# Bias rows stored three heads at a time, and a last block that loads all low words of its weights

## The chip, the core and the metric

The kernel runs on one core of a Trainium2 chip. The metric is the device time of one execution in microseconds. The median of three timed runs of the kernel before is 3193.27 us (3175.7 to 3194.81).

## What is computed

One streaming step of a one-layer hybrid encoder, for a prompt of 2048 rows and a sample of 8 x 16 rows, width 1024, all in float32. Two head groups share one input projection; the bias of this case belongs to the second.

```python
h = rmsnorm(x, norm1_g) * (1 + sc1) + sh1          # modulated by silu(c) @ w_mod + b_mod
proj = h @ w_in                                    # one projection, columns split between the groups
o_a, conv_state, s = mixer_a(...)                  # gated DeltaNet: 4 heads x 128, conv of 4, chunked delta rule
o_b = band_attention(qb, kb, vb, rel_bias)         # 8 heads x 64; 64-row chunks read 8 chunks back
#   rel_bias (8, 320): d = clip(qpos - kpos, -63, 256) + 63;  scores += rel_bias[:, d]
x = x + g1 * (concat(o_a, o_b) @ w_out)
h = rmsnorm(x, norm2_g) * (1 + sc2) + sh2
x = x + g2 * (square(relu(h @ w_up)) @ w_down)
```

## The kernel before

**Products in three passes.** Every weight is cut into a high word (a cast by ScalarE, L175) and a low word (raw minus high), and each product is made of three matmuls: high by high, high by low, low by high (`mm3`, L161 to L164; L519 to L521). `weights` (L166) loads one raw tile of 512 or 528 KB into one of three buffers of the tag raw, casts it into one of four buffers of the tag w, and then gets the low word in one of two ways. The first time that a tile of w_in is used, in block 0, GpSimd subtracts (L182) and SP stores the low word in the DRAM tensor s_w_in (L184). Later the low word is loaded from there (L179).

**Stage one** works through the 17 row tiles in six blocks (`BLOCKS1`): three tiles each, block 0 with the sample tile, block 5 with two. The text counts blocks from one where it says "block two to four" (numbers 1 to 3 in the code) and "last block" (number 5). Each block runs `proj_a` (gate columns, then queries, keys and values of the four heads of group A) and `proj_b` (the columns of group B); blocks 2 and 4 have their `proj_b` put off to the end, so that the order at the end is proj_a of 4, proj_a of 5, then proj_b of 5, 4 and 2. In the last block the flag `mix` makes every other call of `weights` subtract on GpSimd, though the low word is stored: 14 of its 28 tiles. Beside the projections, steps of the delta rule of the block before are interleaved: A is stored and loaded as 32 x 32 pieces (`s_A`, `Z`, `s_U`, A at L666), and VectorE inverts them (`solve32`). While the last blocks run, the first attention tiles already go (`attention_first`), with `bias` read from s_bias.

**The bias rows.** `rel_bias` (L1092) loads the 8 x 320 table into `ext`, writes on VectorE a reversed and extended row of 768 elements for each head on partitions 32 to 39 (L1098 to L1100), stores it in s_ext (L1101), and then copies from DRAM to DRAM, with a step of -1 from row to row, the bias of a tile of 128 rows by 640 columns for each head into s_bias (L1102, 8 x 128 rows of 2,560 bytes) and the sample's 16 by 528 into s_bs (L1103). The tile comes from the tag big, whose two buffers nothing else uses so early.

**What sets the order.** The code is written once in program order; the tile framework then schedules it by a timeline of its own and by when buffers come free, so instructions can go well ahead of where the code has them. `rel_bias` is called ahead of block 1 in the code; its transfers and copies stand in block 0 in the built program. All transfers but a few are issued by SP, in one queue and in order: an issue that must wait holds all those behind it. The engines, too, each work in order.

## Time and profile before

| | |
|---|---|
| timed runs | 3193.27 us median (3175.7 to 3194.81) |
| profiled execution, device time | 3181.62 us |
| profiled execution, span from first to last instruction | 3179.9 us |
| TensorE matmul rows, busy | 3046.9 us, 96% |
| VectorE / ScalarE / GpSimd, busy | 55% / 46% / 20% |
| mean granted clock of TensorE | 0.985 |
| stage one, up to the first product with w_out | about 1114 us of the span |

Busy time is the union of an engine's instructions. A row of waits gives an engine that stood idle, the instruction that it then ran, and the one whose end let it run. Rows of SPq are issues: how long SP took to get a transfer out, not how long it ran. "DMA share" in a stretch is the mean busy share of the 16 transfer engines.

### The profile page before, as it was taken

The page shows a single profiled execution, that of the slowest core. Times are in us where ns is not written, and L with a number is a line of the kernel's source. Part 1 is how long each engine was busy: PE and PEld are TensorE (multiplying, and loading weights), DVE is VectorE, ACT ScalarE, POOL GpSimd, SP SyncE. Part 2 cuts the span into 40 slices and gives each one's busy share as a digit, 9 for nine tenths or more (in the row PEclk, how much of TensorE's full clock was granted, in tenths as well). Part 3 has the DMA queues.
Part 4 walks back from the last instruction along what each step waited for, and adds up shares of the span by engine and source line. Part 5 has one row for each costly group of instructions (what it writes and reads, how often), then busy time and mean ns, then how long its engine had stood idle before and what let it go on. Part 6 is the DMA issues. An engine that isn't in the chain of part 4 may idle for free.

```text
span 3179.9 us, 52984 instructions
## 1 busy us (share of the span) xinstructions
PE 3046.9 (96%) x19649; PEld 2701.7 (85%) x19649; DVE 1764.0 (55%) x4222; ACT 1472.8 (46%) x2803; POOL 644.5 (20%) x517
## 2 busy tenths in 40 slices
PE   6999999999889989999999999999999999999998
PEld 4998989899889878888999888888988877888887
DVE  4775677667878663674356752454745433442223
ACT  3654545555466555545455353444354333333222
POOL 3631211121342247653222200000000000000000
PEclk9999999999999989999999999999999999999999
DMA  8798897888788778876777765666666676856654
GB/s 289 239 294 268 258 284 228 253 250 248 234 268 264 214 229 277 254 250 231 253 238 244 238 214 181 197 193 204 232 198 200 214 236 219 273 173 194 193 190 139
DMA packets 625947, 735.88 MB, mean 231 GB/s; under 512 B 59328, under 2 KB 483248, under 8 KB 623640
## 3 DMA queue, kind: packets, MB, share of 16 engines
q1 hardware_dynamic: 619928, 701.03, 70.1%
q0 software_dynamic: 5760, 31.46, 3.0%
q8 instruction: 155, 2.54, 0.3%
q14 instruction: 104, 0.85, 0.1%
HBM read 619.74 MB, written 115.52 MB: 231 GB/s over the span
## 4 chain that ended last, share of the span: by engine, by line
PE 70%; DMA 13%; DVE 9%; issue 3%; ACT 3%; POOL 1%; SPq 1%; POOLq 0%; ACTq 0%; DVEq 0%
PE psu L1483 7%; PE psu L1482 7%; PE psu L1484 7%; PE psd L164 7%; PE psd L162 7%; PE psd L163 7%; PE psb L163 2%; DMA raw<-in_w_up_dram 2%; PE psb L162 2%; PE psb L164 2%; PE pv L1286 2%; PE psS L1268 2%; PE psq L519 1%; PE psq L521 1%; PE psq L520 1%
## 5 line engine op out<-in xcount | busy, mean ns | idle before, releaser
L175 ACT CAST w<-raw 128x1024 fp32r<-128x1024 f32 (+1 forms) x528 | 552.1, 1047 | 387.1 <-PE psd L164 214.1
L1482 PE MATMUL psu<-hT,w 128*128 128x512 f32 (+2 forms) x1328 | 470.1, 356 | 1.9 <-ACT hT L104 1.7
L1484 PE MATMUL psu<-hT,w 128*128 128x512 f32 (+2 forms) x1328 | 468.5, 354 | 1.4 <-DMA w<-s_w_up 1.4
L1483 PE MATMUL psu<-hT,w 128*128 128x512 f32 (+2 forms) x1328 | 469.2, 354 | 0.4 <-DVE hT L82 0.3
L82 POOL TENSOR_TENSOR w<-raw,w 128x1024 fp32r<-128x1024 f32 (+1 forms) x162 | 391.6, 2427 | 351.3 <-ACT w L175 285.3
L162 PE MATMUL psd<-w,u 128*128 128x512 f32 x1088 | 430.9, 396 | 0.4 <-DVE y L82 0.3
L164 PE MATMUL psd<-w,u 128*128 128x512 f32 x1088 | 429.8, 396 | 0.0
L163 PE MATMUL psd<-w,u 128*128 128x512 f32 x1088 | 426.8, 392 | 2.1 <-POOL w L82 2.1
L79 DVE SCALAR_TENSOR_TENSOR psu<-psu,r 128x512 f32<-128x512 f32 (+2 forms) x160 | 98.9, 618 | 447.0 <-ACT r L92 446.9
L82 DVE TENSOR_TENSOR y<-y,psd 128x512 f32<-128x512 f32 x238 | 162.4, 685 | 260.3 <-PE psd L164 259.3
L1484 PEld LDWEIGHTS psu<-hT,w 128*128 128x128 f32 x1328 | 250.5, 189 | 33.2 <-DMA w<-s_w_up 1.7
L1482 PEld LDWEIGHTS psu<-hT,w 128*128 128x128 f32 x1328 | 250.1, 189 | 33.0 <-ACT hT L104 2.5
L1483 PEld LDWEIGHTS psu<-hT,w 128*128 128x128 f32 x1328 | 250.7, 189 | 31.9 <-issue 1.3
L92 ACT ACTIVATE r<-psu 128x512 f32<-128x512 f32 (+2 forms) x160 | 85.4, 534 | 375.7 <-issue 214.0
L163 PEld LDWEIGHTS psd<-w,u 128*128 128x128 f32 x1088 | 204.6, 188 | 47.8 <-POOL w L82 2.8
L164 PEld LDWEIGHTS psd<-w,u 128*128 128x128 f32 x1088 | 204.2, 188 | 46.4 <-issue 0.4
L162 PEld LDWEIGHTS psd<-w,u 128*128 128x128 f32 x1088 | 204.4, 188 | 43.8 <-DVE y L82 1.0
L162 PE MATMUL psb<-w,hT 128*128 128x256 f32 x816 | 236.0, 290 | 0.9 <-ACT hT L104 0.8
L163 PE MATMUL psb<-w,hT 128*128 128x256 f32 x816 | 234.7, 288 | 0.9 <-DMA w<-s_w_in 0.9
L164 PE MATMUL psb<-w,hT 128*128 128x256 f32 x816 | 233.4, 286 | 1.9 <-DVE hT L82 1.8
L519 PE MATMUL psq<-hT,w 128*128 128x384 f32 (+1 forms) x576 | 196.9, 342 | 8.1 <-ACT ba L499 8.1
L521 PE MATMUL psq<-hT,w 128*128 128x384 f32 (+1 forms) x576 | 193.6, 336 | 0.2 <-DMA w<-s_w_in 0.2
(315 smaller groups left out, 6459.5 us busy)
## 6 DMA issues: line engine op xcount, KB each, us to landing
raw<-in_w_up_dram SPq DMA_DIRECT2D x160, 512.0 KB
raw<-in_w_down_dram SPq DMA_DIRECT2D x160, 512.0 KB
raw<-in_w_in_dram SPq DMA_DIRECT2D x156, 512.0 KB
w<-s_w_down SPq DMA_DIRECT2D x128, 512.0 KB
w<-s_w_in SPq DMA_DIRECT2D x117, 512.0 KB
w<-s_w_up SPq DMA_DIRECT2D x96, 512.0 KB
raw<-in_w_out_dram SPq DMA_DIRECT2D x40, 512.0 KB
x<-in_x_prompt_dram SPq DMA_DIRECT2D x38, 512.0 KB
```

The costliest lines, as they stand in the source:

```text
L79: (eng or self.nc.vector).scalar_tensor_tensor(out, in0, scalar, in1, op0, op1)
L82: (eng or self.nc.vector).tensor_tensor(out, in0, in1, op)
L92: self.nc.scalar.activation(out, in_, func, **kw)
L162: mm(out, lh, rh, start=first, stop=False)
L163: mm(out, lh, rl, start=False, stop=False)
L164: mm(out, ll, rh, start=False, stop=last)
L175: nc.scalar.copy(w[:, 0, 0:n], r)
L519: mm(pc, wh, hT[:, k, 0, 0:T], start=(k == 0), stop=False)
L521: mm(pc, wl, hT[:, k, 0, 0:T], start=False, stop=(k == KT - 1))
L1482: mm(ps[:, c0:c1], wh, h2[:, k, 0, c0:c1], start=(k == 0), stop=False)
L1483: mm(ps[:, c0:c1], wh, h2[:, k, 1, c0:c1], start=False, stop=False)
L1484: mm(ps[:, c0:c1], wl, h2[:, k, 0, c0:c1], start=False, stop=(k == KT - 1))
```

## The change

`rel_bias` takes a range of heads and is called three times, in blocks 1, 2 and 3 of the code, for three, three and two heads. Its tile now comes from the tag htmp (512 columns a partition), so the extended row lies in two parts on two groups of partitions: three copies and a memset for each call, and two stores to s_ext. The s_bias and s_bs stores cover the heads of the call. In `weights` the flag `mix` and its counter go: a low word that is stored is always loaded, so the 14 subtracts of the last block become 14 loads.

```diff
@@ -174,12 +174,11 @@
         nc.sync.dma_start(r.rearrange("p (a b) -> p a b", a=a), src)
         nc.scalar.copy(w[:, 0, 0:n], r)
         key, kept = (name, k0, c0), self.s_w[name]
-        self.turn += self.mix
-        if key in self.stored and not (self.mix and self.turn % 2):
+        if key in self.stored:
             nc.sync.dma_start(w.bitcast(F32)[:, 1, 0:n], kept[self.stored[key]][:, 0:n])
             return v(0), v(1)
         self.tt(w[:, 1, 0:n], r, w[:, 0, 0:n].bitcast(F32), ALU.subtract, eng=nc.gpsimd)
-        if self.keep[name] and key not in self.stored:
+        if self.keep[name]:
             m = sum(k[0] == name for k in self.stored)
             nc.sync.dma_start(kept[m][:, 0:n], w.bitcast(F32)[:, 1, 0:n])
             self.stored[key] = m
@@ -1058,10 +1057,9 @@
             for bi, tiles in enumerate(B):
                 self.bi = bi
                 self.keep["w_in"] = bi == 0
-                if bi == 1:
-                    self.rel_bias()
+                if 1 <= bi <= 3:
+                    self.rel_bias(3 * bi - 3, min(3 * bi, BH))
                 self.drain_to(bi - 2)
-                self.mix = bi == last
                 blk = self.proj_a(tiles, self.hT, B[bi + 1] if bi in LATE else ())
                 if bi == last:
                     break
@@ -1079,7 +1077,6 @@
             rest = [last] + list(LATE)
             self.pace(0.85 * sum(cb(b) for b in rest))
             for b, nb in zip(rest, rest[1:] + [None]):
-                self.mix = b == last
                 self.proj_b(B[b], self.hT, B[nb] if nb is not None else ())
             self.drain()
             nc.sync.dma_start(self.o["gdn_prompt"][0, 0].rearrange("h k v -> k h v"), self.S)
@@ -1089,18 +1086,23 @@
         self.ap2 = self.ctx.enter_context(tc.tile_pool(name="p2att", bufs=1, space=bass.MemoryType.PSUM, side="right"))
 
 
-    def rel_bias(self):
-
-        nc = self.nc
-        x = self.hp.tile([P, D], F32, tag="big", name="ext", bufs=2)
-        ext, rev = x[0:BH, 0:REL], x[32:32 + BH, 0:EXT]
-        nc.sync.dma_start(ext, self.i["rel_bias"][0])
-        nc.vector.memset(rev[:, EXT - 64:], 0.0)
-        nc.vector.tensor_copy(rev[:, EXT - 64 - REL:EXT - 64], ext[:, ::-1])
-        nc.vector.tensor_copy(rev[:, 0:EXT - 64 - REL], bcast(ext[:, REL - 1], 1, EXT - 64 - REL))
-        nc.sync.dma_start(self.s_ext, rev)
-        nc.sync.dma_start(self.s_bias, dram_ap(self.s_ext, P, [[EXT, BH], [-1, P], [1, 640]]))
-        nc.sync.dma_start(self.s_bs, dram_ap(self.s_ext, P, [[EXT, BH], [-1, SL], [1, 528]]))
+    def rel_bias(self, h0, h1):
+
+        nc = self.nc
+        m, k = h1 - h0, EXT - 64 - REL
+        x = self.hp.tile([P, 4, P], F32, tag="htmp", name="ext", bufs=2).rearrange("p a b -> p (a b)")
+        ext, lo, hi = x[0:m, 0:REL], x[32:32 + m], x[64:64 + m, 0:EXT - 512]
+        rev = ext[:, ::-1]
+        nc.sync.dma_start(ext, self.i["rel_bias"][0][h0:h1])
+        nc.vector.tensor_copy(lo[:, 0:k], bcast(ext[:, REL - 1], 1, k))
+        nc.vector.tensor_copy(lo[:, k:], rev[:, 0:512 - k])
+        nc.vector.tensor_copy(hi[:, 0:EXT - 576], rev[:, 512 - k:])
+        nc.vector.memset(hi[:, EXT - 576:], 0.0)
+        nc.sync.dma_start(self.s_ext[h0:h1, 0:512], lo)
+        nc.sync.dma_start(self.s_ext[h0:h1, 512:], hi)
+        o = h0 * EXT + P
+        nc.sync.dma_start(self.s_bias[h0:h1], dram_ap(self.s_ext, o, [[EXT, m], [-1, P], [1, 640]]))
+        nc.sync.dma_start(self.s_bs[h0:h1], dram_ap(self.s_ext, o, [[EXT, m], [-1, SL], [1, 528]]))
 
     def softmax(self, ap, ps, bias, n):
 
@@ -1558,7 +1560,7 @@
     def run(self):
         self.nraw, self.nw = 3, 4
         self.deferred, self.lanes, self.pending, self.fill_rate, self.fill_acc = [], ([], [], []), [0, 0, 0], 0.0, 0.0
-        self.slot, self.mix, self.turn = 0, False, 0
+        self.slot = 0
         self.front, self.solved, self.spent = 0, 0, 0
         self.constants()
         self.phase1()
```

The instructions' order, as the scheduler has built it, is shown in three places. The first is SP's queue in block 0, around the second to sixth weight tile (`s_w_in<-w` is the store of a low word, `sg` the gate's rows). Before:

```order
45 L373 DMA x<-in_x_prompt_dram 128x1024
46 L184 DMA s_w_in<-w 128x1024
47 L174 DMA raw<-in_w_in_dram 128x8x128
48 L1102 DMA s_bias<-s_ext 1024x1x640
49 L1103 DMA s_bs<-s_ext 128x1x528
50 L297 DMA mrow<-in_b_mod_dram 9x256
51 L184 DMA s_w_in<-w 128x1024
52 L174 DMA raw<-in_w_in_dram 128x8x128
53 L373 DMA x<-in_x_prompt_dram 128x1024
```

Of the changed kernel, the same place in the same queue:

```order
43 L372 DMA x<-in_x_prompt_dram 128x1024
44 L183 DMA s_w_in<-w 128x1024
45 L174 DMA raw<-in_w_in_dram 128x8x128
46 L296 DMA mrow<-in_b_mod_dram 9x256
47 L183 DMA s_w_in<-w 128x1024
48 L174 DMA raw<-in_w_in_dram 128x8x128
49 L372 DMA x<-in_x_prompt_dram 128x1024
```

The two stores of the bias are gone from between the weight tiles (as are the ext load and the s_ext store a few rows earlier). The second place is SP's queue early in block two, where the delta rule of the first block stores `s_U` and loads A back. Before:

```order
160 L771 DMA s_U<-Ds 768x1x32 x2
161 L500 DMA s_sg<-sgw 128x256
162 L174 DMA raw<-in_w_in_dram 128x8x128
163 L179 DMA w<-s_w_in 128x1024
164 L174 DMA raw<-in_w_in_dram 128x8x128
165 L179 DMA w<-s_w_in 128x1024
166 L666 DMA A<-s_U 32x4x32 x12
167 L560 DMA s_kt<-kvw 128x128 x3
168 L179 DMA w<-s_w_in 128x1024
```

Of the changed kernel, from the s_ext stores of the first three heads on:

```order
159 L1101 DMA s_ext<-ext 3x512
160 L1102 DMA s_ext<-ext 3x256
161 L499 DMA s_sg<-sgw 128x256
162 L174 DMA raw<-in_w_in_dram 128x8x128
163 L178 DMA w<-s_w_in 128x1024
164 L174 DMA raw<-in_w_in_dram 128x8x128
165 L178 DMA w<-s_w_in 128x1024
166 L174 DMA raw<-in_w_in_dram 128x8x128
167 L1104 DMA s_bias<-s_ext 384x1x640
168 L1105 DMA s_bs<-s_ext 48x1x528
169 L665 DMA A<-s_U 32x4x32 x12
171 L178 DMA w<-s_w_in 128x1024
```

The stores of three heads now stand between the weight tiles and the twelve loads of A. The third place is GpSimd in the last block (`r`, `nk`, `rq` and `zs` are small powers, `X` and `Ds` products of the delta rule). Before:

```order
157 L82 TENSOR_TENSOR w<-raw,w 128x1056
158 L296 MEMSET mrow 128x256
159 L101 TENSOR_TENSOR r<-r,cpow 128x1 x2
160 L101 TENSOR_TENSOR nk<-ssk,cpow 128x12
161 L101 TENSOR_TENSOR rq<-ssq,cpow 128x12
162 L82 TENSOR_TENSOR w<-raw,w 128x1024 x2
163 L82 TENSOR_TENSOR X<-X,nk 128x512
164 L82 TENSOR_TENSOR ta<-low_342,g 128x512
165 L82 TENSOR_TENSOR Ds<-E,strict_339 128x512
166 L82 TENSOR_TENSOR w<-raw,w 128x1024
```

Of the changed kernel, the same place on GpSimd:

```order
154 L101 TENSOR_TENSOR r<-r,cpow 128x1
155 L295 MEMSET mrow 128x256
156 L101 TENSOR_TENSOR nk<-ssk,cpow 128x12
157 L101 TENSOR_TENSOR rq<-ssq,cpow 128x12
158 L101 TENSOR_TENSOR r<-r,cpow 128x1
159 L82 TENSOR_TENSOR X<-X,nk 128x512
160 L82 TENSOR_TENSOR ta<-low_342,g 128x512
161 L82 TENSOR_TENSOR Ds<-E,strict_339 128x512 x2
```

The subtracts of raw tiles are gone from between the small products; on SP a row `w<-s_w_in` stands for each.

## Rows read from the trace of the kernel before

**Rows 1.** The page, part 1: busy us, share of the span, instructions.
```profile
PE 3046.9 (96%) x19649; PEld 2701.7 (85%) x19649; DVE 1764.0 (55%) x4222; ACT 1472.8 (46%) x2803; POOL 644.5 (20%) x517
```

**Rows 2.** Timeline of SP's queue from 50 us: start, us, the issue.
```profile
50.38 0.84 SPq L1102 DMA_DIRECT2D s_bias<-s_ext  x1
51.28 8.49 SPq L1103 DMA_DIRECT2D s_bs<-s_ext  x1
...
61.88 0.39 SPq L174 DMA_DIRECT2D raw<-in_w_in_dram  x1
62.39 5.70 SPq L373 DMA_DIRECT2D x<-in_x_prompt_dram  x1
```

**Rows 3.** Timeline of ScalarE, 62 to 79 us; idle before and releaser in brackets.
```profile
74.43 1.04 ACT L175 CAST w<-raw 128x1024 fp32r<-128x1024 f32 x1 [6.82 <-DMA raw<-in_w_in_dram]
...
78.46 0.17 ACT L499 COPY ba<-psg 128x8 f32<-128x8 f32 x1 [1.75 <-DVE sgw L79]
```

**Rows 4.** Waits of TensorE, 40 to 80 us: total us, times, longest.
```profile
PE psq L519 <- ACT ba L499: 8.1, 1, 8.1
PE psh L346 <- ACT htmp L92: 3.7, 1, 3.7
```

**Rows 5.** Timeline of VectorE, 40 to 49 us.
```profile
40.76 2.60 DVE L1099 COPY ext<-ext 8x320 f32<-8x320 f32 x1 [2.25 <-DMA ext<-in_rel_bias_dram]
43.28 2.48 DVE L1100 COPY ext<-ext 8x384 f32<-8x384 f32 x1
...
45.90 0.40 DVE L89 TENSOR_SCALAR htmp<-psh,modT 128x128 f32<-128x128 f32 x1
...
48.99 0.48 DVE L1051 MEMSET S<- 128x512 f32 x1 [0.17 <-DVE modT L324]
```

**Rows 6.** Busy time by stretch, with its column line.
```profile
core 0: us, PE busy (x) PEld busy (x) DVE busy (x) ACT busy (x) POOL busy (x), PEclk, DMA share, GB/s
56.00:62.00 6.00, 4.52 (x30) 3.84 (x29) 4.50 (x11) 2.92 (x7) 0.56 (x1) 1.00 0.53 209
250.00:260.00 10.00, 8.10 (x50) 7.07 (x48) 2.92 (x6) 5.16 (x11) 0.00 (x0) 0.66 1.02 278
640.00:757.00 117.00, 116.80 (x870) 112.32 (x869) 87.18 (x260) 60.88 (x139) 16.67 (x17) 1.00 0.88 267
757.00:870.00 113.00, 104.83 (x939) 94.07 (x938) 91.94 (x255) 59.79 (x147) 41.54 (x28) 1.00 0.75 218
870.00:935.00 65.00, 58.22 (x493) 52.50 (x491) 47.82 (x142) 37.51 (x80) 29.18 (x26) 0.92 0.87 262
```

**Rows 7.** Timeline of ScalarE, 250 to 404 us.
```profile
251.18 1.04 ACT L175 CAST w<-raw 128x1024 fp32r<-128x1024 f32 x1 [5.63 <-DMA raw<-in_w_in_dram]
...
402.08 0.16 ACT L526 COPY psq<-hist 128x3 f32<-128x3 f32 x1 [2.20 <-PE psq L521]
402.18 1.05 ACT L175 CAST w<-raw 128x1024 fp32r<-128x1024 f32 x1
```

**Rows 8.** Timeline of SP's queue, 228 to 250 us.
```profile
231.54 8.22 SPq L666 DMA_DIRECT2D A<-s_U  x12
```

**Rows 9.** Waits of ScalarE, 480 to 520 us.
```profile
ACT w L175 <- PE psg L164: 2.8, 2, 2.0
```

**Rows 10.** Groups of GpSimd's instructions, 757 to 906 us: busy us, mean ns.
```profile
L82 POOL TENSOR_TENSOR w<-raw,w 128x1024 fp32r<-128x1024 f32 (+1 forms) x14 | 34.0, 2432 | 37.0 <-ACT w L175 31.9 <-DMA mrow<-in_b_mod_dram 4.2 <-POOL ss L101 0.8
```

**Rows 11.** Timeline of all engines, 885 to 892 us.
```profile
884.91 0.41 DVE L82 TENSOR_TENSOR qraw<-qraw,ss 128x256 f32<-128x256 f32 x1
...
889.78 2.42 POOL L82 TENSOR_TENSOR w<-raw,w 128x1024 fp32r<-128x1024 f32 x1 [0.82 <-POOL ss L101]
889.88 2.61 DVE L82 TENSOR_TENSOR qraw<-qraw,ss 128x256 f32<-128x256 f32 x1
892.41 0.41 DVE L313 COPY mrow<-ptm 9x256 f32<-9x256 f32 x1
```

**Rows 12.** Waits of TensorE, 757 to 935 us.
```profile
PE pS L845 <- DVE w L82: 3.3, 1, 3.3
...
PE ptq L554 <- DVE vT L79: 1.6, 2, 1.1
...
PE ptk L1011 <- DVE mrow L313: 1.3, 1, 1.3
PE psg L162 <- DVE kq L79: 1.1, 1, 1.1
```

## The prediction

> **What bounds the kernel now.** The page's busy line comes first: the TensorE matmul rows cover 96% of the span and no other engine is near that [rows 1]. So a microsecond counts only where TensorE waits, or where work that is taken away had been stopping it. I therefore read the waits of TensorE in the two places that the change touches, then the engines that it waits for there, then SP's queue, which issues nearly all transfers in order and stands still whenever one of its issues cannot go out. The reader is to see three things. At the start of the kernel TensorE waits 8.1 and 3.7 us in two single waits, and both lead back to the bias rows [rows 2 to 5]. Where the change puts the bias rows, TensorE is busy but the transfers are close to full. In the last block VectorE is the engine that TensorE waits for, while GpSimd subtracts beside it; those rows come below with their terms.
>
> **What is taken from the start.** SP issues the store of s_bias at 50.38 us; the s_bs store behind it then holds the queue for 8.49 us, and an x load a little later for 5.70, where an ordinary issue takes 0.39 [rows 2]. That is 13.4 us in which SP was held, and the weight load at 61.88 stands behind the first of the two holds. ScalarE, which casts weights in its program order, waits 6.82 us for a raw tile and only then reaches the small copies that free the sums of the first gate tiles [rows 3]; the matmul behind them waits 8.1 us [rows 4]. The other wait, 3.7 us, is that of the transposes that build hT. VectorE had spent 40.76 to 45.8 us on two copies of ext, and the htmp row that the transposes need comes behind them at 45.90 [rows 5]. With both causes gone I take off both waits, 8.1 + 3.7 = 11.8 us, and call it 12. The next thing to be late is the following raw tile, since the weights are cut in two for the first time here and each also has to be stored; that is why I don't go beyond 12. If the transfers of this stretch were the limit by themselves, only the 3.7 us and part of the 8.1 would go: 6 us is the lower bound, about half.
>
> **What is put into blocks two, three and four.** Per block SP gets five transfers (the ext load, two parts of s_ext, s_bias and s_bs), so 15 in all for the old 4. VectorE gets three copies and a memset on two or three partitions. The two copies of before took 2.60 and 2.48 us while GpSimd was subtracting, and a memset 0.48 [rows 5]; GpSimd is nearly idle in the new places (0.00 us busy in 250 to 260 [rows 6]), so I take the lower value, some 2 us for the four on an engine that has idle time there, and nothing on the path. The stores are the question. In 56 to 62 us, with SP held and little but the s_bias rows under way, the transfer engines are busy at a share of 0.53 and move 209 GB/s [rows 6]. So the old store ran at half of the engines' capacity: 2.62 MB (8 heads of 128 rows of 2,560 bytes) at 209 GB/s is 12.5 us. Two readings fit. If half of the engines is what any such store gets, three heads (0.98 MB) take 4.7 us. If it is one engine for each head (8 of 16), three heads get 3 of 16, and 0.98 MB at 3/8 of 209 GB/s takes 12.5 us again; two heads on 2 engines as well. Then the 13 us are not divided by three but paid three times, each time on few engines, and since every weight load is spread over the engines, each load behind the store waits for the slow ones. The exact half speaks for the second reading, and I use it.
>
> The Trainium skill speaks for it too ("DMA: Bandwidth & Descriptors", section "Why a DMA increments its semaphore by 16 and not by 1"): a transfer uses the largest number of engines up to 16 that divides the slowest dimension of both its patterns. The trace agrees as far as it goes, with 0.53 for a pattern whose slowest dimension is 8. By that rule the new stores run on 3, 3 and 2 engines, and the sum is the one made here; by bytes alone each store would be over in about 3 us and the sum would be the first rival's.
>
> What such an event costs TensorE is bounded below by 0 and above by what the same 13 us cost at the start, 8.1 us [rows 4]; three times that is 24.3. Block two is the nearest to the start: its store stands ahead of twelve A loads and the next weight loads on SP. In the kernel before ScalarE already waits 5.63 us for a raw tile at 251 us [rows 7], and TensorE's granted clock falls to 0.66 in 250 to 260 [rows 6]; the A loads, whose issue takes 8.22 us at 231.54 [rows 8], would now go out some 9 us later. I take 6. In block three ScalarE waits 2.20 us for TensorE at 402.08 and the cast behind it waits for nothing [rows 7], and in block four its casts wait 2.8 us for psg, that is for TensorE to give a buffer back [rows 9]: there the raw tiles lie ready, and I take 2 each. Together 10, with 0 and 24.3 kept for the range.
>
> **What changes in the last block.** 14 subtracts of 2,432 ns leave GpSimd, 34.0 us [rows 10]. They cost TensorE nothing directly, but a qraw product on VectorE that takes 0.41 us at 884.91 takes 2.61 at 889.88, while a subtract runs from 889.78, and the mrow copy right behind it at 892.41 [rows 11] ends a wait of TensorE of 1.3 us. The waits of TensorE on VectorE in 757 to 935 that could shrink in this way are 3.3, 1.6, 1.3 and 1.1 us, 7.3 in all [rows 12]. Only the 1.3 is tied to a slow product by its rows; I take 3, bounds 0 and 7.3. In exchange SP issues 14 more loads of 512 KB. A full engine set moves 267/0.88 = 303 GB/s [rows 6], so one load is 1.73 us of it and 14 are 24 us. Eight belong to the first half (757 to 870): a share of 0.75 becomes 0.75 + 13.8/113 = 0.87, which is what 640 to 757 has (0.88) with TensorE busy for 116.80 of 117 us [rows 6]. So these are hidden. Six belong to 870 to 935: 0.87 becomes 0.87 + 10.4/65 = 1.03. The excess over 1 is 2 us, which I take as the cost; if nothing of the loads is hidden there, it is 10.4. The last block together: -3 + 2 = -1, from -7.3 to +10.4.
>
> **The sum.** The profiled execution took 3181.62 us (span 3179.9, 1.7 around it), and the three timed runs 3175.7 to 3194.81 with a median of 3193.27, so a run differs from the next by more than most terms here. 3181.6 - 12 + 10 - 1 = 3178.6, say 3179 us.
>
> **The rivals.** *The stores are hidden.* The loads run ahead far enough in blocks two to four, or the stores use half of the engines whatever the heads. Then the 10 falls away: 3181.6 - 12 - 1 = 3169. For it: TensorE is busy at 116.80 of 117 us in block five with a share of 0.88. Against it: ScalarE's wait of 5.63 us in block two [rows 7].
>
> *Each narrow store costs what the wide one did.* Three times 8.1 us for 10: 3181.6 - 12 + 24.3 - 1 = 3193, slower than before by 11 us. The place is SP's queue in blocks two to four, with ScalarE waiting for raw and the later loads of A, Z and kt late behind the store. It decides from about 4.3 us a store, where three of them take more than the 13 us won elsewhere. For it: the store lasts as long each time by the second reading, and ScalarE and TensorE take their work in order. Against it: at the start nothing had been loaded ahead.
>
> *The last block becomes bound by transfers.* The six loads from 870 us cost their 10.4 us whole: 3179 + 8.4 = 3187. For it: the share of 1.03; against it: the stretch of 870 to 935 has a TensorE that is not full (58.22 of 65 us [rows 6]), part of it for VectorE.
>
> **How the numbers follow.** I give the forecast 0.43 (3170 to 3188), the hidden stores 0.25, the full price 0.22, the transfer-bound last block 0.10. The predicted time is 3179 us. For the range the ends are 3181.6 - 12 - 7.3 = 3162 below and, with the full price and a start that gives only 6, 3181.6 - 6 + 24.3 + 2 = 3202 above; 6 us more above, half of what the median of before lies over its profiled execution, make it 3162 to 3208. About 1%, 32 us, is what a measurement of this kernel can tell from no change. No case reaches 32 us on its own; two at their ends together, or a shift in how the scheduler interleaves blocks one to five, could. So faster by over 1% gets 0.04, within 1% 0.90, slower by over 1% 0.06.
>
> **What would show it.** In the new profile the waits of 8.1 and 3.7 us between 40 and 80 us should be gone and the first matmuls of block one's queries and keys start some 12 us earlier. In blocks two to four an s_bs issue of about 8 us should stand behind each s_bias store, with a low transfer share around it; issues of under 2 us would mean that the engines' number does not follow the heads. A wait of ScalarE for raw of over 10 us in block two would confirm its 6 us, none would refute it. In the last block GpSimd should show no subtract of raw and VectorE no product of 2.6 us, with a share near 1 from 870 us on. The prediction is wrong if the start keeps its 8 us, or if any one store costs TensorE more than the 8.1 us that bounds it here.

## The result and the profile after

The changed kernel takes 3231.74 us (median of four runs, 3225.42 to 3242.65) against 3190.07 us of the kernel before (3175.7 to 3194.81): a ratio of 1.0142, 95% interval 1.0098 to 1.0186. It is slower by some 42 us. The forecast was 3179 us, range 3162 to 3208. The profiled execution of the changed kernel has a span of 3223.7 us, 43.8 more than before.

The page, part 1, of the changed kernel (busy us, share, instructions) answers to [rows 1]:

```profile
PE 3071.3 (95%) x19649; PEld 2723.8 (84%) x19649; DVE 1752.9 (54%) x4231; ACT 1472.6 (46%) x2803; POOL 612.4 (19%) x503
```

TensorE runs the same 19,649 matmul rows and is busy 24.4 us longer; the other 19.4 us are waits. The longer busy time goes with the clock: the mean granted clock is 0.975 after 0.985.

To see where the 43.8 us come from I numbered the 13,872 projection matmuls (psg, psq, psb and the later products with weights) in both traces and compared the start of the same one. The changed kernel is 11.5 us ahead at the 137th (in the head), 2.5 at the 145th, 2.9 us ahead at the 1,009th (225.5 against 228.4 us, block two), 33.1 us behind at the 2,305th (565.4 against 532.4, block four), 32.8 behind at the 3,169th (749.6 against 716.8), 51.3 behind at the 4,897th (1152.8 against 1101.5, the end of stage one), and 43.8 behind at the end. So 36 of the 43.8 us are lost in blocks two to four, between 225 and 565 us: 30.0 of it is time in which TensorE stands (38.3 us there after 8.3), and 5.9 is busy time for the same matmuls. The 18.5 us between the 3,169th and the 4,897th are busy time alone (TensorE stands for 23.0 us after 23.4), and stage two gives back 7.5. Each figure compares one execution with one other: between before and E15 (below), whose TensorE order is the same, the distance at the same points is up to 13.7 us. The three long waits stand far outside of that: the three profiles of null edits stand for 8.8 to 10.3 us between the 1,009th and the 2,305th, where the change stands for 38.3. TensorE's waits there, 225 to 560 us of the changed kernel (total us, times, longest):

```profile
PE psq L520 <- DMA w<-s_w_in: 10.1, 1, 10.1
PE ptO L875 <- DVE z L79: 10.0, 1, 10.0
PE ptT L788 <- DMA A<-s_U: 9.3, 2, 9.0
PE psh L345 <- DVE modT L323: 3.5, 1, 3.5
```

One wait of 9 to 10 us for each of the three stores. The beginnings of the one in block two are on SP's queue (start, us, issue), where [rows 8] is the answering row of before:

```profile
229.65 2.13 SPq L1104 DMA_DIRECT2D s_bias<-s_ext  x1
231.84 6.96 SPq L1105 DMA_DIRECT2D s_bs<-s_ext  x1
238.84 14.57 SPq L665 DMA_DIRECT2D A<-s_U  x12
```

SP is held by the s_bs issue for 6.96 us, as the forecast said ("about 8"); then the twelve small A loads, whose issue took 8.22 us before, take 14.57, and TensorE stands for 9.03 us, until 250.44, for the first A. Busy time by stretch of the changed kernel, with its column line; the answering rows of before are in [rows 6]:

```profile
core 0: us, PE busy (x) PEld busy (x) DVE busy (x) ACT busy (x) POOL busy (x), PEclk, DMA share, GB/s
...
77.00:84.00 7.00, 5.89 (x26) 5.89 (x27) 4.94 (x15) 4.41 (x16) 4.44 (x3) 0.54 0.25 76
...
820.00:830.00 10.00, 10.00 (x57) 8.27 (x55) 3.29 (x8) 3.58 (x8) 0.00 (x0) 0.50 0.74 240
890.00:940.00 50.00, 44.24 (x353) 40.03 (x353) 36.63 (x136) 27.28 (x59) 10.65 (x12) 0.94 1.05 354
...
241.00:250.00 9.00, 0.41 (x2) 0.09 (x1) 0.35 (x1) 0.00 (x0) 0.00 (x0) 0.71 0.24 80
411.00:421.00 10.00, 0.18 (x2) 0.00 (x0) 2.41 (x9) 0.23 (x2) 1.04 (x1) 0.72 0.69 220
...
494.00:511.00 17.00, 15.68 (x150) 13.37 (x150) 9.88 (x31) 9.89 (x21) 1.12 (x2) 0.50 0.76 235
```

From 241 to 250 us all five engines all but stand, and so do most of the transfer engines: a share of 0.24 and 80 GB/s is the store of three heads and the small pieces beside it. In block three (411 to 421 us) other loads go on beside the store, at a share of 0.69, and it is the low word that TensorE needs next that is late. The waits are not waits for raw tiles alone. ScalarE's waits in 225 to 262 and in 400 to 430 us:

```profile
ACT kvw L556 <- DMA s_kt<-kvw: 16.7, 1, 16.7
...
ACT w L175 <- DMA raw<-in_w_in_dram: 0.2, 1, 0.2
...
ACT w L175 <- DMA raw<-in_w_in_dram: 11.6, 2, 10.3
```

and in block four the chain runs through GpSimd, which waits for an X load, and VectorE, which waits for GpSimd (the timelines of GpSimd and of VectorE, 515 to 556 us):

```profile
548.96 1.04 POOL L82 TENSOR_TENSOR X<-X,nk 128x512 f32<-128x512 f32 x1 [24.57 <-DMA X<-s_vt]
...
551.01 0.99 DVE L82 TENSOR_TENSOR zs<-zs,rq 128x4 f32<-128x4 f32 x1 [13.43 <-POOL zs L101]
```

### The profile page after: what moved, and what is told of

The parts are those of the page before. It is cut to its first block, busy times and chain, and to the rows that moved or that the text cites. A ratio compares the mean times of both kernels' runs of the same rounds, so it can differ in the third digit from the quotient of the medians.

```text
span 3223.7 us, 53038 instructions
## 1 busy us (share of the span) xinstructions
PE 3071.3 (95%) x19649; PEld 2723.8 (84%) x19649; DVE 1752.9 (54%) x4231; ACT 1472.6 (46%) x2803; POOL 612.4 (19%) x503
## 4 chain that ended last, share of the span: by engine, by line
PE 52%; DMA 4%; DVE 4%; ACT 1%; issue 1%; POOL 1%; SPq 0%; POOLq 0%; ACTq 0%; DVEq 0%
PE psu L1485 7%; PE psu L1484 7%; PE psu L1486 7%; PE psd L164 7%; PE psd L162 7%; PE psd L163 7%; PE pv L1288 2%; PE psS L1270 2%; PE pso L162 1%; DMA raw<-in_w_up_dram 1%; PE psP L1278 1%; PE pso L163 1%; PE pso L164 1%; DVE y L82 1%; DMA raw<-in_w_down_dram 1%
## 5 line engine op out<-in xcount | busy, mean ns | idle before, releaser
L82 POOL TENSOR_TENSOR w<-raw,w 128x1024 fp32r<-128x1024 f32 (+1 forms) x148 | 359.4, 2438 | 315.8 <-ACT w L175 259.2
L520 PE MATMUL psq<-hT,w 128*128 128x384 f32 (+1 forms) x576 | 194.9, 338 | 10.1 <-DMA w<-s_w_in 10.1
```

The lines of the kernel that those rows point to most:

```text
L82: (eng or self.nc.vector).tensor_tensor(out, in0, in1, op)
L520: mm(pc, wl, hT[:, k, 0, 0:T], start=False, stop=(k == KT - 1))
```

## The experiments

Theory N: a store of bias rows occupies one transfer engine for each head, about 13 us whatever the number of heads, and what the loads behind it bring comes late by that much. Its main rivals are the loads of the last block (L), the bytes of a store (B), and the order of instructions that any edit makes anew (R). Ratios are to the kernel before, with 95% intervals.

| | edit | median us | ratio |
|---|---|---|---|
| E1 | bias part alone | 3232.92 | 1.0132 (1.0098 to 1.0167) |
| E2 | last block's loads alone | 3199.37 | 1.0026 (1.0009 to 1.0044) |
| E3 | the change, stores over 16 engines | 3203.94 | 1.0048 (1.0033 to 1.0063) |
| E4 | the change, stores on GpSimd's queue | 3230.08 | 1.0129 (1.0079 to 1.018) |
| E5 | E3 with the last block as before | 3205.8 | 1.0066 (1.004 to 1.0092) |
| E6 | eight heads in block two | 3195.87 | 1.0042 (1.0027 to 1.0058) |
| E7 | four calls of two heads | 3229.33 | 1.0142 (1.0108 to 1.0175) |
| E8 | before, store over 16 engines | 3186.55 | 1.0008 (0.999 to 1.0026) |
| E9 | the change, decay sums later | 3213.67 | 1.0088 (1.0069 to 1.0106) |
| E10 | E3, decay sums later | 3210.25 | 1.0074 (1.0056 to 1.0092) |
| E11 | eight heads in block two, 16 engines | 3198.15 | 1.0037 (1.0021 to 1.0054) |
| E12 | the same in block five | 3209.68 | 1.0074 (1.0054 to 1.0095) |
| E13 | before, no store of bias rows | 3207.66 | 1.0069 (1.0047 to 1.0092) |
| E14 | E13 with the last block's loads | 3212.1 | 1.0076 (1.0054 to 1.0098) |
| E15 | before, a memset in block two | 3187.28 | 1.0 (0.9982 to 1.0017) |
| E16 | before, a memset in block three | 3191.53 | 1.0022 (1.0006 to 1.0038) |
| E17 | before, a memset in block five | 3183.38 | 0.999 (0.9975 to 1.0005) |
| E18 | the change, a memset in block five | 3228.94 | 1.0136 (1.0112 to 1.016) |

### Which part of the change it is: E1 and E2

E1 is the changed kernel with `mix` and its counter kept; E2 is the kernel before with only these lines:

```diff
-        self.turn += self.mix
-        if key in self.stored and not (self.mix and self.turn % 2):
+        if key in self.stored:
```

> Only the bias part of the change: stored three heads at a time in blocks two, three and four; the last block treats its weights as before. Theory N (each store of three heads is moved by three DMA engines at 77 GB/s, some 13 us for 960 KB, and what stands behind it in SP's one queue comes late): the three TensorE waits of about 10 us in blocks two, three and four stand here as in the changed kernel, with some microseconds at half clock behind each. Block four ended 33 us behind before in the changed kernel, so 3190 + 33 = 3223 us, ratio about 1.010. Rival L (the loss is made in the last block, by its loads): the waits stand, but the time is that of before plus the 10 us less 12 us of the prediction, about 3188 us, ratio 1.00.

> Only the other part: the bias is stored once, in the head, as before; the last block loads every low word and subtracts none. Theory N: the last block costs the rest of the 42 us, at most 10 us, since its DMA share of about 1.05 in 890 to 940 us is only a little over what the engines can bring: 3192 to 3200 us, ratio 1.000 to 1.003. Rival L: it costs what the changed kernel lost between the end of block four and the end of stage one, some 18 us: 3208 us, ratio 1.006.

The bias part alone is as slow as the whole change (1.0132 and 1.0142; 1.010 had been expected), with the same three waits, here of 8.0, 10.6 and 10.7 us. The loads alone cost 8 us (1.0026), but with the bias part in place they add nothing that can be told: E1 against the change, E3 against E5 and E13 against E14 differ by +0.10, -0.18 and +0.07%. So L falls as the cause of the 42 us. What the loads cost beside the bias part stays open, for the profiles of the three pairs don't agree on it: between the 3,169th and the 4,897th projection matmul the change takes 11.1 us longer than E1, E3 takes 5.3 less than E5, and E14 as long as E13. In E2 the loads do fill the transfer engines, and then leave them idle (stretches of E2):

```profile
870.00:900.00 30.00, 29.15 (x246) 26.42 (x244) 24.44 (x88) 17.56 (x36) 8.65 (x9) 1.00 1.05 358
...
960.00:990.00 30.00, 25.12 (x178) 23.55 (x177) 26.72 (x83) 16.84 (x40) 7.73 (x11) 0.92 0.40 121
```

### Engines, queue, or bytes: E3, E4, E6 and E7

E3 makes sixteen the outermost dimension of a store. The table is written in sixteen copies, and each copy serves eight of a head's 128 rows; a store is issued for each head (the code is cut: the second part of the table and s_bs are changed in the same way):

```diff
-        nc.sync.dma_start(self.s_ext[h0:h1, 0:512], lo)
+        nc.sync.dma_start(self.s_ext[:, h0:h1, 0:512].rearrange("a h c -> h a c"), bcast(lo, 1, 16))
...
-        nc.sync.dma_start(self.s_bias[h0:h1], dram_ap(self.s_ext, o, [[EXT, m], [-1, P], [1, 640]]))
+        for h in range(h0, h1):
+            nc.sync.dma_start(self.s_bias[h].rearrange("(a b) c -> a b c", a=16),
+                              dram_ap(self.s_ext, h * EXT + P, [[BH * EXT - 8, 16], [-1, 8], [1, 640]]))
...
```

> The changed kernel, but each store of bias rows is made to run over sixteen DMA engines: the extended table is stored in sixteen copies, and each copy serves eight of a head's 128 rows, so the outermost dimension of a store is 16 in place of 3. Bytes, place in the program and number of heads per block are those of the change; one store per head in place of one for three. Theory N: the 77 GB/s stretch behind each store is gone (2.9 MB at some 300 GB/s take 3 to 4 us a block), the three 10 us waits fall under 4 us, and the time falls from 3232 by 25 to 33 us to about 3203 us, ratio to before about 1.004. Rival S (the new place of the stores and the order that the scheduler made around them, whatever engines move them): waits and time stay as in the changed kernel, about 3230 us, ratio 1.012.

The time falls by 0.9%, to 3203.94 us as forecast. SP's queue in block two of E3:

```profile
233.69 3.60 SPq L1105 DMA_DIRECT2D s_bias<-s_ext  x3
237.34 0.60 SPq L1106 DMA_DIRECT2D s_bs<-s_ext  x1
237.98 9.12 SPq L665 DMA_DIRECT2D A<-s_U  x12
```

The s_bs issue is back at 0.60 us and the A loads at 9.12. The wait for A in block two is down to 0.9 us and the wait for z in block four is gone. For a weight's low word TensorE still waits 3.2 us in block two and 6.5 in block three (waits of TensorE, 225 to 560 us of E3), more than the 4 that I had expected:

```profile
PE psq L520 <- DMA w<-s_w_in: 9.7, 2, 6.5
```

E4 puts both stores on another queue, GpSimd's, and leaves their shape as it is (three packets of the first store are under way at once in its trace, as in the changed kernel):

```diff
-        nc.sync.dma_start(self.s_bias[h0:h1], ...
+        nc.gpsimd.dma_start(self.s_bias[h0:h1], ...
```

> The changed kernel, with the two stores of bias rows (the 128-row and the 16-row one) of each of the three calls issued on GpSimd's queue in place of SyncE's. They still run over three engines. Theory N in its form with the queue (what hurts is that everything behind the store waits in the same queue): the three waits shrink to under 4 us, time about 3203 us, ratio 1.004. In its form with the engines (the loads behind need the three engines too, whichever queue they come from): the waits stay at 5 to 10 us, time 3215 to 3230 us. What can go the other way: GpSimd itself waits for the table's store and stands still for 2 to 4 us three times, and its subtractions come late.

The time stays (1.0129). GpSimd's two issues cost 1.31 and 0.64 us and SP is no longer held by s_bs, but its twelve A loads then take 21.09 us to issue. Timelines of GpSimd and SP, and a stretch, of E4:

```profile
228.92 1.31 POOL L1104 DMA_DIRECT2D s_bias<-s_ext  x1
230.23 0.64 POOL L1105 DMA_DIRECT2D s_bs<-s_ext  x1
...
229.31 21.09 SPq L665 DMA_DIRECT2D A<-s_U  x12
...
238.00:248.50 10.50, 0.27 (x2) 0.00 (x0) 0.48 (x1) 0.00 (x0) 0.00 (x0) 0.61 0.22 77
```

TensorE waits 10.3 us for A in block two, with 77 GB/s moved meanwhile, and 8.7 us for z in block four. In block three the wait of 10 us for a low word is gone (TensorE waits 4.4 us for VectorE's kq there), but block four then loses more, and by the 2,305th matmul E4 is 35.1 us behind, the changed kernel 33.1. So it is not the place in SP's queue that costs the time: a load on SP's queue is late though the store is on another, which leaves the transfer engines that both need.

E6 calls the new code once, for eight heads, in block two; E7 calls it four times for two heads, in blocks two to five. Both leave the last block as before.

```diff
-                if 1 <= bi <= 3:
-                    self.rel_bias(3 * bi - 3, min(3 * bi, BH))
+                if bi == 1:                                   # E6
+                    self.rel_bias(0, BH)
+                if 1 <= bi <= 4:                              # E7
+                    self.rel_bias(2 * bi - 2, 2 * bi)
```

> The new code of the bias rows, but called once, for all eight heads, in block two; the last block as before. The store then runs over eight engines and brings 8/3 of the bytes of one call of the change. Theory N (a store lasts as long as one engine needs for one head, whatever the number of heads): one TensorE wait of about 9 us near 250 us, none at 420 and 553 us, so a third of the loss that e1 showed: 3190 + 43/3 = about 3204 us, ratio 1.004. Rival B (the wait goes by the bytes of a call): a wait of 8/3 x 9 = 24 us near 250 us and the same loss as e1, about 3225 to 3233 us.

> The new code called four times, for two heads each, in blocks two to five; the last block as before. Each store runs over two engines. Theory N: each of the four stores keeps its engines as long as one of three heads does, some 13 us, so a fourth TensorE wait of up to 10 us comes in block five, and the time is that of e1 plus up to 14 us: 3233 to 3247 us, ratio 1.013 to 1.018. Rival B (bytes): each wait is two thirds as long, four together 27 us in place of 29: 3230 us or a little less.

By bytes E6 should have had a wait of 24 us; its longest in blocks two to four is 5.1 and the ratio is 1.0042, as N gave, though N's 9 us for the wait was too high. Behind the store of eight heads the transfers keep a share of 0.54 and 209 GB/s, the figures that the wide store of before had in the head [rows 6]. A stretch and a wait of E6:

```profile
236.00:245.00 9.00, 9.00 (x56) 7.72 (x55) 5.24 (x9) 3.75 (x10) 0.00 (x0) 1.00 0.54 209
...
PE ptT L789 <- DMA A<-s_U: 7.7, 4, 5.1
```

In E7 the stretch in which block two waits shows 58 GB/s, and a fourth store in block five brings its own wait of 8.2 us (a stretch, SP's queue and waits of TensorE, 225 to 780 us, of E7):

```profile
240.00:249.00 9.00, 0.29 (x2) 0.00 (x0) 0.00 (x0) 0.00 (x0) 0.00 (x0) 0.67 0.19 58
...
724.08 0.65 SPq L1107 DMA_DIRECT2D s_bias<-s_ext  x1
724.77 4.59 SPq L1108 DMA_DIRECT2D s_bs<-s_ext  x1
...
PE ptq L554 <- DVE kq L79: 13.5, 5, 8.2
PE ptT L789 <- DMA A<-s_U: 11.9, 6, 8.7
```

The wait of block five ends at 760 us; VectorE stood 8.22 us there for a Z load, and in the kernel before TensorE has no such wait. The waits of blocks two and three are about as long as with three heads (8.7 and 9.2 us against 9.0 and 10.1), that of block four is half as long (5.3). E7's time of 3229 us decides nothing: N gave 3233 or more, B 3230 or a little less. What decides is how long a store lasts, and the packets in the traces show it. A row of a head is one packet of 2,560 bytes, so a head has 128. From the first of a store's packets to the end of its last:

| store | packets | mostly under way at once | us |
|---|---|---|---|
| before, eight heads | 1,024 | 8 | 13.3 |
| the change, three, three and two heads | 384, 384, 256 | 3, 3, 2 | 13.9, 13.2, 13.3 |
| E7, two heads, four times | 256 each | 2 | 13.2, 12.8, 13.8, 13.4 |
| E6, eight heads in block two | 1,024 | 8 | 14.4 |
| E3, three, three and two heads | 384, 384, 256 | up to some 16 | 3.7, 5.2, 3.9 |

Outside of E3 a packet takes 102 to 108 ns in the mean, and 128 of them one behind the other 13 to 14 us: a store lasts as long as one engine needs for one head, whether it carries two heads or eight. N stands and B falls.

### What the head gave: E8, E9 and E10

E8 makes the single store of before run over sixteen engines, by the same copies.

> The kernel before with its single store in the head made over sixteen engines in place of eight, by the sixteen copies of e3. Theory N: the store lasts half as long, the 8.1 us wait of TensorE on the ba chain at 78 us and the 3.7 us wait at 47 us get shorter by up to 6 us together; the sixteen copies of the table (393 KB) cost some of it: 3184 to 3192 us, ratio 0.998 to 1.001. Rival: the head's waits have another cause than how long the store keeps its engines, and the time stays within 1 us of before, or goes up by the copies' 2 to 4 us.

No change that can be told (1.0008, inside what both theories gave). The 8.1 us wait [rows 4] shrinks to 3.5, and another of 7.0 us appears 17 us earlier (waits of TensorE, 30 to 100 us of E8):

```profile
PE psg L164 <- DVE hT L82: 7.0, 1, 7.0
PE psq L519 <- ACT ba L499: 3.5, 1, 3.5
```

E8 is no clean test of the head, though. Its store shares the engines with other loads and takes 14.2 us from first to last packet, no less than the 13.3 of before. And its table is a narrow store itself: the sixteen copies are written with the eight heads as outermost dimension, 128 packets of 3,072 bytes with at most eight under way at once, from 44.7 to 53.0 us.

In the changed kernel both waits of [rows 4] are gone from the head as well, and what took their place is the wait of the decay sums for VectorE's g chain (waits of TensorE, 30 to 100 us of the changed kernel), with a granted clock of 0.54 in 77 to 84 us; the kernel before had 0.50 in 75.7 to 82.5, at its own wait:

```profile
PE psd L615 <- DVE g L82: 4.7, 1, 4.7
```

In the kernel before these sums stand 54 rows of TensorE's order later, at 94.20 us, and wait for nothing. E9 and E10 make them stand there again:

```diff
         g = blk["g"]
+        if not blk["base"]:
+            self.stt(g, blk["kq"][0][:, 1, 0:n * AH].rearrange("p (t h) -> p t h", h=AH), 0.0, g, ALU.mult, ALU.add)
```

> The changed kernel with one edit in block one: the decay sums (psd<-g) are made to depend on the second kq tile (g gets 0 times some of its elements added), so that they stand behind 249 TensorE rows, as in the kernel before, and not behind 199. Theory H (the head did win the 12 us, and the early decay sums gave most of it back by their 4.75 us wait for the g chain at 78 us and the half clock behind it): the wait goes, the 144th projection matmul comes 8 us earlier, and the time falls from 3232 by 5 to 9 us, ratio to before about 1.011. Rival K (the gain is lost to something else in the head, so that it is gone by 100 us in any case): no gain behind 100 us, ratio as the changed kernel's, 1.014.

> e3 (stores over sixteen engines) with e9's later decay sums. By theories N and H together both parts of the loss in stage one's first blocks are mended: ratio of e3 (1.005) less 5 to 9 us, 1.002 to 1.003. If H is wrong, 1.005.

In E9 the wait only changes its name (waits of TensorE, 30 to 100 us of E9):

```profile
PE ptq L553 <- DVE kq L79: 5.9, 1, 5.9
```

VectorE makes kq too, and is not done with it. At the 1,009th projection matmul E9 is 4.3 us ahead of before, the changed kernel 2.9: later sums were worth at most 1.4 us there, not 8 (E18, whose TensorE order is that of the changed kernel, is 1.5 us ahead). E9 is faster than the change (1.0088 against 1.0142), which neither theory gave. The two profiles are 11.7 us apart at the end: 1.4 from the head, 4.4 from block four, where the wait for z (10.0 us) became one of 5.9 for another tile, 7.7 from the 3,169th matmul to the 4,897th, where the granted clock is 0.944 against the change's 0.937, and -1.8 from the rest. E10 with the same edit is not faster than E3 (1.0074 against 1.0048). So theory H falls, and of K it holds that the head's gain is gone by 100 us: once the bias rows are gone, VectorE's chain is due some 5 us later, and that is what the head waits for.

### Versions that should have won: E5, E11, E12 and E13 with E14

> The sixteen-copy stores of e3 in blocks two to four, with the last block's weights as before (half the low words subtracted): e3 without the second part of the change. If the two parts add, as e2 (the second part alone: 3199 us against 3190) says, 3204 less 9 gives 3195 us, ratio 1.002. If they do not (e1, without the second part, took 3233 us against 3232 of the whole change), 3204 us, ratio 1.005.

> All eight heads stored once, in block two, over sixteen engines (sixteen copies), decay sums later as in e9, last block as before. By N and H: 2.6 MB over sixteen engines keep them some 8 us, a TensorE wait of 3 to 5 us in block two and none in three and four; head 8 to 10 us earlier: 3183 to 3190 us on a base of 3188, ratio 0.998 to 1.001. If the head's gain does not last: 1.002 to 1.004, as e6.

> As e11, with the one call in block five in place of block two: there the DMA engines are as busy (share 0.91 to 0.95 at 670 to 757 us against 0.87 to 1.10 at 200 to 300 us), so the same wait is expected: ratio 0.998 to 1.001. If the place alone decides, it differs from e11 by more than 0.3%.

None is faster than before. E11 still loses 6 us in block two (a wait of 4.8 us on VectorE's vT at 238 us), E12 has none of the waits of blocks two to four and is 1.5 us ahead at the 2,449th matmul, and then waits 8.2 us for a low word in block five. A wide store is still 2.6 MB, and its table some 0.4 MB, among the weight loads wherever it lies; how much of the two losses that is was not separated from their changed order.

E13 leaves the store out: the loads of bias rows read the sixteen copies of the table themselves (one of three loads is shown).

```diff
-            nc.sync.dma_start(bias, self.s_bias[h, :, 640 - W:])
+            nc.sync.dma_start(bias, dram_ap(self.s_ext, h * EXT + P + 640 - W, [[BH * EXT - 8, 16], [-1, 8], [1, W]]))
...
```

> The kernel before with no store of bias rows anywhere: the table is stored in sixteen copies in the head (393 KB), and every load of bias rows reads the copies (eight rows of a head from each), so the 2.6 MB store and its 79 KB companion are gone. Same results. Theory H (the head's 12 us are real, but another chain, on VectorE, comes due some 5 us earlier): the 8.1 us wait at 78 us goes or shrinks, the head gains 4 to 6 us and keeps it, since no store comes later: 3182 to 3185 us on a base of 3188, ratio 0.998 to 0.999. If all 12 us hold: 0.996. If the gain is lost later: 1.000 to 1.003.

> e13 with the second part of the change: the last block loads every low word and subtracts none. If these loads cost what e2 showed, e13 plus 9 us, ratio 0.3% above e13's; if nothing, as in the changed kernel against e1, the same ratio as e13.

This is the largest surprise: without any store of bias rows the kernel is slower by 0.7%. The head does not gain at all. The wait of 8.1 us is gone, but VectorE stands 4.44 us for an x tile between the two halves of hT (timeline of VectorE and a wait of TensorE, E13). The statistics of x stand between halves of hT in the kernel before too, and wait for nothing there. What differs is the x load: SP got it out in 0.33 us at 47.99 before, and is held by it for 4.31 us at 47.69 in E13 (timeline of SP, E13):

```profile
47.69 4.31 SPq L373 DMA_DIRECT2D x<-in_x_prompt_dram  x1
...
58.44 1.29 DVE L378 BATCH_NORM_STATS2 bst<-x 128x6 f32<-128x512 f32 x2 [4.44 <-DMA x<-in_x_prompt_dram]
...
PE psg L164 <- DVE hT L82: 6.3, 1, 6.3
```

Under way at that time is the table, which here has sixteen copies and, as in E8, the eight heads as outermost dimension: 128 packets from 44.76 to 52.89 us, at most eight at once, and all transfers together move 102 GB/s from 47 to 52 us where the kernel before moves 252 and the changed kernel 328. E13 has thus put another narrow store into the head, and its head is no test of one without; the changed kernel's is. At the 145th projection matmul E13 is 3.2 us behind the kernel before. The other 20 us come in steps of 1 to 4 us between 450 and 1,250 us, with no wait of over 4.3 us among them; their cause stays open.

### How much is the order alone: E15 to E18

```diff
+                if bi == 1:                                   # E15; 2 in E16; 4 in E17 and E18
+                    z = self.hp.tile([P, 4, P], F32, tag="htmp", name="idle", bufs=2)
+                    nc.vector.memset(z[0:8, 0, 0:8], 0.0)
```

> The kernel before with one memset of 8x8 elements of an unused tile on VectorE, written at the start of block two (behind the bias store's code). It costs about 0.1 us of VectorE; the scheduler makes a new order for it. Theory R (any edit's new order costs the kernel 0.3 to 0.7% against the order of the kernel before): ratio 1.003 to 1.007. Theory O (the order is no cost by itself): 0.999 to 1.001.

> As e15, with the memset at the start of block three. Theory R: 1.003 to 1.007, and different from e15 by its own order. Theory O: 0.999 to 1.001.

> As e15, with the memset at the start of block five. Theory R: 1.003 to 1.007. Theory O: 0.999 to 1.001.

> The changed kernel with the memset of e17. Its three narrow stores are as they were, so the three 10 us waits stand; by both theories it is 1.0142 with the scatter that e15 to e17 show: theory R 1.010 to 1.018, theory O 1.013 to 1.015.

In E15 and E17 the order of TensorE's instructions came out as that of the kernel before, so they say only that a null edit measures 0.999 to 1.000. In E16 the memset moved some of it (668 of the 19,649 matmul rows stand at another place in the trace), and that alone is worth 0.2% (1.0006 to 1.0038). E18 confirms the three waits (7.6, 9.8 and 10.0 us) and the loss. Theory R is thus neither needed for the change's 42 us nor excluded for the 0.4 to 0.7% that E6, E11, E12 and E13 lose: in these 1,703 to 3,223 rows stand at another place. In E8 1,097 do, and its time is that of before. What this remainder is made of stays open.

## Why the prediction was wrong

**The head, -12.** Both waits went, and at the 137th matmul the changed kernel was 11.5 us ahead: the reading of SP's queue was right so far. At the 145th it was 2.5 us ahead. The step that failed is "With both causes gone I take off both waits", with its lower bound of 6 and its guess that a raw tile would be late next. Late next was VectorE, 4.7 us, at a granted clock of 0.54; 2.9 us were left in block two. E9 put the decay sums back and found another tile of VectorE's late, 5.9 us, so it is a chain and not one misplaced instruction. E8 and E13 add nothing to this, since both write a narrow table into the head. The waits of [rows 4] were where the head's slack ended, not what the head would give up. I had the rows to see it: VectorE's chain in the head could have been dated from the trace of before and laid against the earlier start of TensorE.

**Three stores, +10.** The number of engines was read rightly: of the two readings that fit a share of 0.53, the second, one engine for each head, is what two, three and eight packets under way at once and some 13 to 14 us for each store show. The rule of the Trainium skill ("DMA: Bandwidth & Descriptors", section "Why a DMA increments its semaphore by 16 and not by 1") says the same. The trace agrees: the shares were 0.19, 0.24 and 0.54 with two, three and eight as the slowest dimension. E3, with sixteen, gets back 28 of the 42 us. The step that failed, and the largest part of the miss, is the term behind it, 6 + 2 + 2 us; measured were waits of 9.0, 10.1 and 10.0 us and 36 us lost from block two to block four. The reason given for 2 was "there the raw tiles lie ready". That looked at one of the transfers behind the store. TensorE waited for A pieces in block two, a stored low word in block three and, through GpSimd and VectorE, an X tile in block four, each loaded shortly before its use. The sign named for the 6 us, a wait of ScalarE for raw of over 10 us in block two, did not come: it is 0.2 us there. The upper bound of 8.1 us a store was no bound either: it was the wait that one such event had left in the head, where other waits ran beside it.

**What the sum had no term for.** Of the 36 us lost in blocks two to four 5.9 are busy time, and so are all 18.5 of the stretch from 750 to 1153 us. The forecast priced waits only. [rows 6] had one stretch of low clock behind a wait (0.66 in 250 to 260 us); the changed kernel runs at a granted clock of 0.50, that is at 1.2 GHz, from 494 to 511 us, where the kernel before had 1.00, and again from 820 to 830. The 18.5 us are clock and not other work: between the 3,169th and the 4,897th matmul both kernels run the same TensorE rows but for three (3,111 before, 3,114 after), and the granted clock over the stretch is 0.987 before and 0.937 after. Part of it is scatter, for the null edits E15 to E17 take 3.9 to 7.7 us longer there than the one profile of before. What lowered the clock further stays open: E1, without the last block's loads, loses 7.4 us there, E2, with them alone, 17.3, but E5, without them, 19.6.

**The last block, -1.** GpSimd's subtracts of raw are gone from it, VectorE's 64 qraw products there last 0.40 to 0.43 us each and none 2.6, and the share is 1.05 in 890 to 940 us, all as said. Alone the two edits of the last block cost 8 us (E2), inside the bounds of -7.3 to +10.4; beside the bias part the times of three pairs show no cost, and their profiles don't agree on one.

**The rivals and chances.** "Each narrow store costs what the wide one did" was the right mechanism and named the right place, with 0.22; its 3193 us is too low by 9 us of head (2.9 for 12), 11.7 in blocks two to four (36.0 for 24.3), and the 10.7 behind them. With the measured sizes the sum is 3181.6 - 2.9 + 36.0 + 10.7 (from 33.1 to 43.8 us behind) = 3225.4, the profiled execution's own time, as it has to be, since the sizes are read from that execution. "Slower by over 1%" had 0.06, since no single case reached 32 us; the note that "two at their ends together" could was right and weighed too little: both ends hung on one assumption, that a wait seen in the head is what an event costs or gives anywhere.

## What to carry to other kernels

Cost a transfer by the number of engines that its outermost dimension gives it, and by how long one of them works: cutting such a store into three with fewer heads each keeps its length and pays for it three times. Cost a cure in the same way: the table in sixteen copies was a narrow store of 8 us itself. Then date every transfer that needs those engines while the store runs, not only the weight loads, and take a wait's removal as a gain only as far as the next chain's end has been dated too. A kernel whose order a scheduler makes needs a null edit as a measure: here an 8x8 memset moved 0.2%.

## What the runs showed that was not expected

A transfer from DRAM to DRAM whose slowest dimension is 2, 3 or 8 lasted 12.8 to 14.4 us in all three cases, with two, three or eight packets of 2,560 bytes under way at once. Issued from GpSimd in place of SyncE the store of three heads still had three under way and took 14.2 us, and the time stayed (1.0129 against 1.0142): loads on one queue were late behind a store on the other. Reading rows with a step of -1 from sixteen copies of a table makes such a transfer wide (E3, s_bs issue 0.60 us in place of 6.96). And a store can be narrow where it is meant to cure one: the 0.39 MB of the table took 8.1 us in E13, and leaving the 2.6 MB of bias rows out won nothing (1.0069).
